# Key transposes one tile in two, earlier key loads and delayed output stores in a hard-max attention kernel

## The chip, the cores and the metric

The kernel runs on one core of one Trainium2 chip. Its time is device microseconds (us) for one execution. Before the change it was 474.49 us (median of 3 runs, 474.13 to 474.59).

Engines: PE is TensorE (PEld its weight loads), DVE is VectorE, ACT is ScalarE, POOL is GpSimd, SP is SyncE.

## The reference

```python
# B=4, Sq=Sk=4096, D=128, float32
logits = np.matmul(q, k.transpose(0, 2, 1))
best = np.argmax(logits, axis=-1)
return v[b_idx, best, :]
```

For each of the 16384 queries, the kernel finds the key with the largest dot product and returns that key's row of v.

## The kernel before

The queries are worked on in 128 tiles of 128 rows, 32 tiles per batch (tile t belongs to batch t // 32). For a tile TensorE makes 4 products of 1024 columns each. `pd` products are differences of key pairs, of which ScalarE takes the absolute value (A); `psn` products are sums to which TensorE then adds A. ScalarE turns the first psn of a tile into E, and VectorE's `fold` combines the second psn with E into W. `top` then takes the eight largest values of W per row.

```python
def dpart(t, x):
    ps = pp.tile([P, 1024], FP32, tag="u", name=f"pd_{t}_{x}")
    mm(ps, t, 1 + 2 * x, True)
    A = ep.tile([P, 1024], FP16, tag=f"A{x}", name=f"A_{t}_{x}")
    nc.scalar.activation(out=A, in_=ps, func=AF.Abs)              # L198
    ...
def spart(t, x):
    ps = pp.tile([P, 1024], FP32, tag="u", name=f"psn_{t}_{x}")
    mm(ps, t, 2 * x, False)                                      # L189
    for n in range(2):
        nc.tensor.matmul(out=ps[...], lhsT=identh, rhs=A[...], start=False, stop=True)   # L208
    if x == 0:
        nc.scalar.activation(out=E, in_=ps, func=AF.Relu, scale=QSCALE)                  # L211
    else:
        E_t[t] = (E_t[t], ps)

def screen(t):          # TensorE's order in one tile
    dpart(t, 0)         # "pd0"
    spart(t - 1, 0)     # "psn0"
    dpart(t, 1)         # "pd1"
    spart(t - 1, 1)     # "psn1"

def fold(t):
    E, ps = E_t.pop(t)
    nc.vector.scalar_tensor_tensor(out=W..., in0=ps, scalar=QSCALE, in1=E,
                                   op0=OP.mult, op1=OP.max)       # L224
```

All these products, and the key transposes, take PSUM buffers from one pool of four, under one tag:

```python
pp = ctx.enter_context(tc.tile_pool(name="ps", bufs=4, space=bass.MemoryType.PSUM))
```

The keys of the next batch must be transposed while this batch runs. This is done in 16 pieces per batch, each of which takes a buffer of the same pool, 8 small matmuls and a copy by ScalarE:

```python
def unit_k(b, i):
    ps = pp.tile([P, 256], FP32, tag="u", name=f"uk_{b}_{i}")
    ...                                                          # matmuls, L163 and L164
    nc.scalar.activation(out=kT[b % 2][:, c:c + 256], in_=ps, func=AF.Copy)   # L167
```

For each tile GpSimd then gathers rows of key differences (`kg`), VectorE makes their dot products (`prod` and what follows), picks the winner, GpSimd gathers the rows of v, and SyncE stores them. Near tiles 80 to 85 a segment of extra work for close cases (the "flags") also takes two PSUM buffers, `fp` and `fq`. The main loop before, cut:

```python
units += [(x - 1, x - NQT + 8 + 3 * i // 2, unit_k, b, i) for i in range(16)]   # from tile 8 of a batch, 2 tiles of 3
for it in range(T):
    b, qt = it // NQT, it % NQT
    if 2 <= qt < 10:
        load_part(b + 1, qt - 2)        # 8 key loads of the next batch
    elif 10 <= qt < 18:
        load_part(b + 1, qt - 2)        # 8 query loads of the next batch
    ...                                 # one transpose unit, if one is due
    if it > 0:
        screen(it)
    if it >= 1:
        fold(it - 1)
    ...
```

## Time and profile before

| | before |
|---|---|
| time, median | 474.49 us |
| profiled span, clock | 472.4 us, 0.944 |
| VectorE busy in 110 us from 30, 140, 250 us | 108.20, 108.11, 108.38 us |
| VectorE's waits, 42 to 420 us | 3.4 us (8 waits) |
| start of the last fold; from there to the end | 419.06 us; 53.3 us |

Two lines from the profile's page of the kernel before: the busy time of each engine over the span (share, instructions), and the group of the fold (busy us, mean ns | idle before it, and what ended most of that).

```profile
PE 381.7 (81%) x1840; PEld 168.9 (36%) x1840; DVE 417.8 (88%) x845; ACT 380.7 (81%) x438; POOL 305.6 (65%) x345
...
L224 DVE SCALAR_TENSOR_TENSOR W<-psn,E 128x1024 int16<-128x1024 f32 x128 | 166.4, 1300 | 15.1 <-ACT E L211 12.1
```

VectorE is the busiest engine, but 88% is an average over a start, a middle and a tail. The windows view of the kernel before shows the middle alone:

```profile
core 0: us, PE busy (x) PEld busy (x) DVE busy (x) ACT busy (x) POOL busy (x), PEclk, DMA share, GB/s
30.00:140.00 110.00, 104.36 (x509) 46.67 (x508) 108.20 (x183) 107.02 (x129) 66.61 (x76) 1.00 0.46 94
140.00:250.00 110.00, 99.89 (x487) 44.63 (x486) 108.11 (x197) 102.23 (x123) 80.14 (x90) 1.00 0.55 117
250.00:360.00 110.00, 99.86 (x475) 43.56 (x473) 108.38 (x217) 101.57 (x117) 78.07 (x81) 1.00 0.43 105
```

VectorE is busy all but 1.6 to 1.9 us of each 110. What it waits for is in the view of waits, here for VectorE from 42 to 420 us in the kernel before (us in total, times, longest):

```profile
DVE W L224 <- PE psn L208: 3.0, 7, 0.9
DVE prod L260 <- DMA kg<-k,cand: 0.4, 1, 0.4
```

So the fold waited 7 times for the psn sum from TensorE, 3.0 us in all, and a dot product once for a gather. VectorE's timeline of the kernel before places them; five of the eight are shown (start, duration; in brackets the idle time before and what ended it):

```profile
164.52 0.56 DVE L260 TENSOR_TENSOR prod<-kg,natq 128x768 f16<-128x768 f16 x1 [0.45 <-DMA kg<-k,cand]
...
176.44 1.30 DVE L224 SCALAR_TENSOR_TENSOR W<-psn,E 128x1024 int16<-128x1024 f32 x1 [0.43 <-PE psn L208]
...
180.03 1.30 DVE L224 SCALAR_TENSOR_TENSOR W<-psn,E 128x1024 int16<-128x1024 f32 x1 [0.39 <-PE psn L208]
...
265.56 1.31 DVE L224 SCALAR_TENSOR_TENSOR W<-psn,E 128x1024 int16<-128x1024 f32 x1 [0.56 <-PE psn L208]
...
283.61 1.30 DVE L224 SCALAR_TENSOR_TENSOR W<-psn,E 128x1024 int16<-128x1024 f32 x1 [0.95 <-PE psn L208]
```

The waits up to 189 us fall where the batch 2 keys are transposed (tiles 40 to 62), those at 241, 266 and 284 us where the batch 3 keys are transposed; at the last two the flags run as well. The Trainium skill (Perfetto Trace Analysis, "Optimization Strategy") says that the same gap repeating on the engine that should be saturated can mean that there isn't enough PSUM for the next tile, and names buffer count and tile sizes.

### The profile page before, as it was taken

Reading aid. Unit: us, or ns where it says so; the run is one execution under the profiler, and the core shown is the slowest. Engines: PE = TensorE matmul, PEld = TensorE weight load, DVE = VectorE, ACT = ScalarE, POOL = GpSimd, SP = SyncE. Lnnn points to the kernel's source line nnn. Section 1 sums busy time; section 2 is a strip of 40 time slices with the busy share of each in tenths; the row PEclk is TensorE's granted clock in tenths of the full one; section 3 lists DMA queues with packets and bytes.
Section 4 is the critical chain, followed back from the end, with each engine's and each line's share of the span. In section 5 each row is a group of like instructions: output and inputs, shape, how many; then the busy total and the mean of one; then the engine's idle time right before and its main releaser. Section 6 shows DMA issues by size and latency. Waiting matters only on the chain. (4 is left out here: it accounts for less than half of the span.)

```text
span 472.4 us, 6274 instructions
## 1 busy us (share of the span) xinstructions
PE 381.7 (81%) x1840; PEld 168.9 (36%) x1840; DVE 417.8 (88%) x845; ACT 380.7 (81%) x438; POOL 305.6 (65%) x345
## 2 busy tenths in 40 slices
PE   7899999999898889999888979999999889920000
PEld 4444444443343334443333434443333333300000
DVE  4288999999999999999999999999999999998400
ACT  1999999999998899999998889999999888920000
POOL 9025544666787876666878765667777567777740
PEclk9999999999999999999999999999999999975555
DMA  7914564143455946242666736142333132324320
GB/s 134 211 32 87 108 115 93 56 119 63 119 94 125 193 87 147 57 124 65 134 133 156 113 108 97 55 114 65 118 89 109 52 94 58 110 73 121 98 82 5
DMA packets 40777, 47.43 MB, mean 100 GB/s; under 512 B 24200, under 2 KB 32395, under 8 KB 40736
## 3 DMA queue, kind: packets, MB, share of 16 engines
q0 software_dynamic: 18464, 30.97, 31.1%
q1 hardware_dynamic: 22272, 16.00, 12.8%
q8 instruction: 15, 0.25, 0.2%
q14 instruction: 26, 0.21, 0.2%
HBM read 39.59 MB, written 12.19 MB: 110 GB/s over the span
## 5 line engine op out<-in xcount | busy, mean ns | idle before, releaser
L198 ACT ACTIVATE A<-pd 128x1024 f16<-128x1024 f32 x256 | 259.1, 1046 | 18.3 <-PE pd L189 17.8
L245 POOL DMA_INDIRECT kg<-k,cand x128 | 127.2, 994 | 103.9 <-DVE p L264 25.0
L224 DVE SCALAR_TENSOR_TENSOR W<-psn,E 128x1024 int16<-128x1024 f32 x128 | 166.4, 1300 | 15.1 <-ACT E L211 12.1
L189 PE MATMUL pd<-kT,qT 128*128 128x512 f16 x512 | 152.1, 378 | 17.4 <-ACT A L198 15.5
L189 PE MATMUL psn<-kT,qT 128*128 128x512 f16 x512 | 151.8, 377 | 15.4 <-ACT A L198 10.8
L189 PEld LDWEIGHTS <-qT 128*128 128x128 f16 x1024 | 98.4, 97 | 166.1 <-issue 77.9
L228 DVE MAX8 TOP<-W 128x8 f32<-128x1024 f32 x128 | 156.2, 1220 | 0.0
L208 PE MATMUL psn<-A,identh 128*128 128x512 f16 x512 | 152.0, 378 | 0.0
L302 POOL DMA_INDIRECT vr<-in_v_dram,win x128 | 125.5, 980 | 39.0 <-issue 35.0
L211 ACT ACTIVATE E<-psn 128x1024 int16<-128x1024 f32 x128 | 132.8, 1038 | 6.7 <-PE psn L208 5.9
L208 PEld LDWEIGHTS <-identh 128*128 128x128 f16 x512 | 49.5, 97 | 60.8
L260 DVE TENSOR_TENSOR prod<-kg,natq 128x768 f16<-128x768 f16 x64 | 35.0, 549 | 1.5 <-DMA kg<-k,cand 1.5
L264 DVE TENSOR_TENSOR p<-prod 128x384 f16<-128x384 f16 x64 | 22.3, 350 | 0.0
L269 DVE TENSOR_REDUCE D<-p 128x6 f32<-128x192 f16 x64 | 21.4, 338 | 0.0
L167 ACT ACTIVATE kT<-uk 128x256 f16<-128x256 f32 x48 | 20.0, 416 | 0.9 <-PE uk L164 0.9
L163 PE MATMUL uk<-identh,natk 128*128 128x128 f16 x96 | 15.8, 218 | 0.6 <-ACT A L198 0.6
L63 POOL DMA_DIRECT2D natk<-in_k_dram x26 | 15.7, 604 | 0.9 <-POOLq L763 0.8
L267 DVE TENSOR_TENSOR p<-p 128x192 f16<-128x192 f16 x64 | 15.7, 247 | 0.0
L66 POOL DMA_DIRECT2D natq<-in_q_dram x26 | 15.4, 594 | 0.1
L460 PE MATMUL fp_e<-n_e,tri 128*128 128x1 f32 x2 | 0.6, 362 | 16.4 <-DVE n_e L458 16.4
L164 PEld LDWEIGHTS <-natk 128*128 128x128 f16 x96 | 9.3, 97 | 7.7 <-issue 5.5
L163 PEld LDWEIGHTS <-natk 128*128 128x128 f16 x96 | 9.3, 97 | 5.6
(148 smaller groups left out, 142.4 us busy)
## 6 DMA issues: line engine op xcount, KB each, us to landing
out_dram<-vr SPq DMA_DIRECT2D x14, 512.0 KB, 3.2
k<-kd SPq DMA_DIRECT2D x8, 384.0 KB, 4.5
natk<-in_k_dram POOLq DMA_DIRECT2D x24, 128.0 KB, 3.8
natq<-in_q_dram POOLq DMA_DIRECT2D x24, 128.0 KB, 3.3
kg<-k,cand POOLq DMA_INDIRECT x128, 2.7
vr<-in_v_dram,win POOLq DMA_INDIRECT x128, 2.5
natk<-in_k_dram POOLq DMA_DIRECT2D x2, 512.0 KB, 7.0
out_dram<-vr SPq DMA_DIRECT2D x4, 256.0 KB, 2.3
```

The costliest lines, as they stand in the source:

```text
L163: nc.tensor.matmul(out=o, lhsT=natk[b % 2][:, h, 4 * m + x, :], rhs=identh, start=True, stop=False)
L189: nc.tensor.matmul(out=ps[:, n * 512:(n + 1) * 512], lhsT=qT[b % 2][:, qt * P:(qt + 1) * P], rhs=kT[b % 2][:, u * 1024 + n * 512:u * 1024 ...
L198: nc.scalar.activation(out=A, in_=ps, func=AF.Abs)
L208: nc.tensor.matmul(out=ps[:, n * 512:(n + 1) * 512], lhsT=identh, rhs=A[:, n * 512:(n + 1) * 512], start=False, stop=True)
L211: nc.scalar.activation(out=E, in_=ps, func=AF.Relu, scale=QSCALE)
L224: nc.vector.scalar_tensor_tensor(out=W_t[t % NW].bitcast(I16)[:, 1::2], in0=ps, scalar=QSCALE, in1=E, op0=OP.mult, op1=OP.max)
L228: nc.vector.max(out=TOP[:, t, :], in_=W_t[t % NW].bitcast(FP32))
L245: near_q.append(lambda j=j: nc.gpsimd.indirect_dma_start(out=kg[:, j].rearrange("p f d -> p (f d)"), out_offset=None, in_=k16[t0 // NQT], ...
L260: nc.vector.tensor_tensor(out=prod, in0=kg, in1=natq[b % 2][:, x - b * NQT:x - b * NQT + m, :].unsqueeze(2).to_broadcast([P, m, 3, P]), op ...
L264: nc.vector.tensor_tensor(out=p1, in0=prod[:, :, :, 0:64], in1=prod[:, :, :, 64:128], op=OP.add)
L269: nc.vector.tensor_reduce(out=d[:, x - c0:x - c0 + m, 1:4], in_=p2, axis=AX_X, op=OP.add)
L302: late_q.append(lambda j=j: nc.gpsimd.indirect_dma_start(out=vr[:, j, :], out_offset=None, in_=v_flat, in_offset=IOA(ap=win[:, j:j + 1], a ...
```

## The change

Its intent is to spread work. The transposes for batches 2 and 3 go over the whole batch before, at one tile in two from its tile 1 on. Those for batch 1 begin at tile 6 instead of 8. The key loads begin sooner (batch 1's at tile 0 instead of 2; those of batches 2 and 3 at tile 18 of the last batch but one, instead of tile 2 of the batch before), and each output store is issued two tiles behind its last gather.

```diff
+    wait_q = []
...
         while late_q and late_q[0] in stores:
-            late_q.pop(0)()
+            wait_q.append((clock[0] + 2, late_q.pop(0)))
+    clock = [0]
+    def put_out(now):
+        while wait_q and wait_q[0][0] <= now:
+            wait_q.pop(0)[1]()
     def issue(it):
         n = 0
+        clock[0] = it
+        put_out(it)
...
-        units += [(x - 1, x - NQT + 8 + 3 * i // 2, unit_k, b, i) for i in range(16)]
+        units += [(x - 1, x - NQT + (6 + 3 * i // 2 if b == 1 else 1 + 2 * i), unit_k, b, i) for i in range(16)]
...
-        if 2 <= qt < 10:
-            load_part(b + 1, qt - 2)
+        if it < 8:
+            load_part(1, it)
         elif 10 <= qt < 18:
             load_part(b + 1, qt - 2)
+        elif 18 <= qt < 26:
+            load_part(b + 2, qt - 18)
...                            # at the end, the last stores are put out at once (late_now)
```

More of the change, by code (lines that the diff above doesn't have):

```diff
@@ L710, in flush, with late_now @@
             near_q.pop(0)()
+    def late_now(n):
+        take_late(n)
+        put_out(1 << 20)
     screen(T)
@@ L746 @@
         drain([p], "cnt" if last else None)
-    flags_last(T // 2, T, lambda: drain([p]), take_late)
+    flags_last(T // 2, T, lambda: drain([p]), late_now)
     man.__exit__(None, None, None)
```

## The prediction

> What bounds the kernel: VectorE. The windows view has it busy 108.2, 108.1 and 108.4 us of the 110 us windows that begin at 30, 140 and 250 us. ScalarE has 101.6 to 107.0, TensorE 99.9 to 104.4, so both have some slack. Outside lie a start (first fold at 19.5 us) and a tail from 420 us, where GpSimd issues gathers back to back (0.94 us and a 0.30 us gap each) until 455 us.
>
> What can be gained. VectorE's waits between 25 and 420 us sum to only about 5.9 us: 2.5 us in the ramp before 40 us (fold waits for ScalarE's E), 0.45 us for a gather at 164.5 us, and seven waits of the fold for TensorE's sum (psn), 2.95 us in all, at 170, 176, 180, 189, 241, 266 and 284 us. Most of these lie where key transposes are made at two tiles of three. A transpose takes one of four PSUM buffers and a ScalarE copy of about 0.4 us; the timeline at 163 to 177 us shows the next matmul waiting about 0.5 us for ScalarE and ScalarE then 0.46 us for that matmul.
>
> What the change moves. Counts stay: 48 transposes, 24 key loads, the same gathers and stores. In batches 2 and 3 the transposes come at one tile in two, so a pause always lies between two; I expect most waits at 170 to 190 us and part of those at 266 and 284 us to go: minus 2 us. The last two also involve the flag segment's PSUM tiles, which stay. Batch 1's transposes begin at tile 6 instead of 8, in the ramp where ScalarE is full (2.75 us per tile, against about 3.05 where VectorE sets the pace): plus 0.5 us.
> Key loads cost GpSimd about 0.58 us and a 0.3 us gap each. Eight leave tiles where GpSimd is full (no slack from 130 to 174 us) for later ones, and eight of batch 3 move to about 72 to 97 us, where GpSimd has about 8 us of slack: the 0.45 us wait may go, nothing else on the critical path.
> The stores' delay frees the sync queue: the store there was followed by bunched query transposes at 179 and 281 us, needed much later: 0. The Trainium skill (DMA: Bandwidth & Descriptors, Issuing engines are not separate DMA queues) says all issuers share the same 16 engines, so it saves no bandwidth; the queues' shares here sum to 44%. One 512 KB store moves into the tail, near the flags' gathers: 0 to plus 0.5 us.
>
> Sum: about minus 2 us, 472.4 us. Range 470.3 to 474.7. Faster by over 2% 0.01, within 2% 0.98, slower 0.01; over 2% would need 9.5 us, more than all of VectorE's waits in that stretch.
>
> What would show it. Waits for psn at 165 to 190 us at most 0.4 us in sum; fold-for-E waits before 45 us larger by about 0.5 us; VectorE's busy total unchanged within 1 us (417.8); last fold about 2 us earlier; time from last fold to end unchanged within 0.7 us; batch-3 key loads at 72 to 97 us.
>
> What would make it wrong. If those waits come from the key differences on VectorE or from late gathers rather than the transposes' density, they stay; if GpSimd, full from 397 us on, sets the end by itself, a VectorE gain is lost; if GpSimd lags in tiles 16 to 26, new gather waits appear.

## More of the kernel before

A buffer holds 1024 float32 (4 KiB) per partition. The Trainium skill (PSUM — Partial Sum Buffer, "PSUM: the matmul accumulator") gives PSUM 16 KiB in each partition, so four such buffers fill it, and a fifth is not to be had; no run here tests that.

## The result, and the profile after

| | before | after |
|---|---|---|
| time, median of 4 runs | 474.54 us (474.13 to 474.59) | 471.19 us (471.06 to 471.39) |
| profiled span, clock | 472.4 us, 0.944 | 469.4 us, 0.941 |
| start of the last fold | 419.06 us | 416.07 us |
| from there to the end | 53.3 us | 53.3 us |

The ratio is 0.9932, with a 95% interval of 0.9914 to 0.9949. The change is worth 3.35 us by the medians.

The same two lines of the page, for the kernel after:

```profile
PE 381.8 (81%) x1840; PEld 169.8 (36%) x1840; DVE 417.2 (89%) x845; ACT 379.7 (81%) x438; POOL 305.8 (65%) x345
...
L224 DVE SCALAR_TENSOR_TENSOR W<-psn,E 128x1024 int16<-128x1024 f32 x128 | 167.6, 1309 | 13.1 <-ACT E L211 11.9
```

No engine has noticeably more or less to do: the totals differ by 1.0 us at most. The idle time before the fold is 2.0 us less. The windows of the kernel after:

```profile
30.00:140.00 110.00, 104.73 (x521) 47.30 (x519) 108.05 (x180) 107.26 (x131) 67.23 (x76) 1.00 0.50 95
140.00:250.00 110.00, 102.09 (x499) 45.62 (x497) 109.21 (x201) 104.20 (x125) 79.42 (x87) 1.00 0.57 114
250.00:360.00 110.00, 100.08 (x465) 43.16 (x464) 110.00 (x221) 101.42 (x115) 79.99 (x83) 1.00 0.47 106
```

VectorE has become full in the third window (110.00) and nearly so in the second (109.21). VectorE's waits from 42 to 420 us in the kernel after:

```profile
DVE W L224 <- PE psn L208: 0.6, 2, 0.3
DVE prod L261 <- DMA kg<-k,cand: 0.2, 1, 0.2
```

Two waits of the fold are left, at 182 and 186 us; those of the flags are gone.

Comparing the starts of the 128 folds in the two traces shows where the time came from. Kernel after minus kernel before: +0.29 us at tile 0, +0.52 at tiles 8 to 47, -0.46 at tiles 56 to 71, -1.57 at tiles 80 to 83, -2.97 from tile 91 on. So the ramp cost 0.23 us, batch 1's tiles gained 0.98 us, and batch 2's tiles (with the flags) 2.5 us. The +0.29 at the first fold is not the change: the run with the stores alone changed, which begins with the same program, had +0.35. The clock between 10 and 15 us differs as well: 1.00 in the profile of before and 0.66 in both others. Over all eight profiles from this chip the two go together: the first fold starts at 19.35 to 19.71 us in the four where that clock is 1.00, and at 19.82 to 19.93 us in the four where it is 0.66 to 0.70. The Trainium skill (TensorE: Matmul & The Clock Gate, Part 1) says that the clock's activity window runs freely, so that the warm-up varies from run to run.

### The profile page after: what moved, and what is told of

Its sections match the earlier page's. It is cut to its first block, busy times and chain, and to the rows that moved or that the text cites. A ratio compares the mean times of both kernels' runs of the same rounds, so it can differ in the third digit from the quotient of the medians.

```text
span 469.4 us, 6266 instructions
## 1 busy us (share of the span) xinstructions
PE 381.8 (81%) x1840; PEld 169.8 (36%) x1840; DVE 417.2 (89%) x845; ACT 379.7 (81%) x438; POOL 305.8 (65%) x345
## 5 line engine op out<-in xcount | busy, mean ns | idle before, releaser
L224 DVE SCALAR_TENSOR_TENSOR W<-psn,E 128x1024 int16<-128x1024 f32 x128 | 167.6, 1309 | 13.1 <-ACT E L211 11.9
L189 PE MATMUL pd<-kT,qT 128*128 128x512 f16 x512 | 152.3, 379 | 15.1 <-ACT A L198 14.4
```

The costliest lines, as they stand in the source:

```text
L189: nc.tensor.matmul(out=ps[:, n * 512:(n + 1) * 512], lhsT=qT[b % 2][:, qt * P:(qt + 1) * P], rhs=kT[b % 2][:, u * 1024 + n * 512:u * 1024 ...
L224: nc.vector.scalar_tensor_tensor(out=W_t[t % NW].bitcast(I16)[:, 1::2], in0=ps, scalar=QSCALE, in1=E, op0=OP.mult, op1=OP.max)
```

## The experiments

The theories are these.

- Density: the waits come because transposes stand at two tiles of three, with too few tiles between them to recover. This is what the prediction said.
- GpSimd: key loads crowd the gathers, so that the rows of key differences arrive late and VectorE's later waits follow from that.
- Stores: output stores held up the sync queue, or moved the tail.
- Buffers (where an expectation says D, it is this one): what matters is which product of a tile is given the PSUM buffer that the fold freed long ago. The framework makes that choice when the program is built, and the change merely made it choose otherwise.

### 1. The parts of the change, one at a time

The key loads alone moved, as in the change, transposes and stores left as before:

```diff
-        if 2 <= qt < 10:
-            load_part(b + 1, qt - 2)
+        if it < 8:
+            load_part(1, it)
         elif 10 <= qt < 18:
             load_part(b + 1, qt - 2)
+        elif 18 <= qt < 26:
+            load_part(b + 2, qt - 18)
```

> The kernel before with only the new key load schedule. Theory A (the waits come from transposes made at two tiles of three): no gain, 474.0 to 475.0 us, VectorE's fold waits for psn between 130 and 290 us still 2 us or more in sum. Theory B (the waits come from GpSimd being full of gathers plus loads): the waits follow the loads; most of the gain appears, 471.5 to 473.0 us, the waits at 165 to 190 us shift to where GpSimd has no slack, those at 241 to 284 us shrink below 0.6 us. Theory C (stores that block the sync queue): no gain, 474.0 to 475.0 us.

Measured: 474.54 us against 474.44 for the kernel before, ratio 1.0005 (0.9992 to 1.0017). VectorE's waits, 42 to 420 us, of this run:

```profile
DVE W L224 <- PE psn L208: 3.3, 7, 1.0
```

The gather wait is gone, and the seven waits of the fold are there as before. The loads alone do nothing for the time.

Loads and transposes as in the change, stores at once as before. The edit is the change with one line's effect taken back:

```diff
-            wait_q.append((clock[0] + 2, late_q.pop(0)))
+            late_q.pop(0)()
```

> The changed kernel without the delayed stores. Theory A and theory B: 471.2 us within 0.4, like the changed kernel. Theory C: 472.5 us or more, with waits for psn just after a store that holds back several query transposes.

Measured: 471.24 us (median of 6 runs, 471.05 to 473.52), ratio 0.9944 (0.9928 to 0.9959). VectorE's waits, 42 to 420 us:

```profile
DVE W L224 <- PE psn L208: 0.8, 3, 0.3
```

This is the change's whole gain: its median lies 0.05 us from the change's own.

The stores alone delayed, loads and transposes as before:

```diff
-            late_q.pop(0)()
+            wait_q.append((clock[0] + 2, late_q.pop(0)))
```

> The kernel before with only the stores issued two tiles behind their last gather. Theories A and B: 474.5 us within 0.4. Theory C: 472.5 us or less, the waits at 180 and 284 us gone. If the tail suffers from the store that moves into it, the time from the last fold to the end grows from 53.3 us by up to 0.5 us.

Measured: 474.81 us, ratio 1.0007 (0.9994 to 1.002). VectorE's waits, 42 to 420 us:

```profile
DVE W L224 <- PE psn L208: 3.4, 7, 1.0
```

The stores are worth nothing.

So, by elimination, the gain belongs to the schedule of the transposes. They were not moved alone: in the change the first transpose for batch 2 comes at tile 33, and the old schedule loads those keys at tiles 34 to 41. The next question is why.

### 2. Is it GpSimd, after all?

The kernel before, with the key and query loads for batches 1 to 3 spread at one tile in two, and the transposes as dense as before:

```diff
-        if 2 <= qt < 10:
-            load_part(b + 1, qt - 2)
-        elif 10 <= qt < 18:
-            load_part(b + 1, qt - 2)
+        if 2 <= it < 10:
+            load_part(1, it - 2)
+        if b >= 1 and qt in (0, 2, 4, 6):
+            load_part(b + 1, 4 + qt // 2)
+        elif 8 <= qt < 24 and qt % 2 == 0:
+            load_part(b + 1, 8 + (qt - 8) // 2)
+        elif qt in (24, 26, 28, 30):
+            load_part(b + 2, (qt - 24) // 2)
```

> The kernel before with its transposes still at two tiles of three and old stores, but with every load of batches 1 to 3 at one tile in two (batch 1's key loads stay as they are), so that GpSimd is never full for long. Theory A: 474.0 to 475.0 us, psn waits between 130 and 290 us still 2 us or more. Theory B: 471.0 to 472.8 us, at most 0.6 us of such waits between 130 and 200 us, and GpSimd keeps some slack in each 10 us of 130 to 200 us.

Measured: 474.65 us, ratio 1.0006 (0.9993 to 1.0019). VectorE's waits, 42 to 420 us:

```profile
DVE W L224 <- PE psn L208: 3.0, 7, 1.0
DVE W L224 <- PE uk L164: 0.4, 1, 0.4
```

The gather no longer waits, but the next fold, at 166.57 us, now waits 0.4 us for TensorE instead, and every fold starts within 0.05 us of where it started before. So the 0.45 us gather wait of the kernel before had hidden a wait for TensorE of the same size: taking it away gains nothing. The GpSimd theory falls.

### 3. What TensorE waits for

The timeline of TensorE in the kernel before, around the transpose of tile 47 (the last line is pd0 of tile 47):

```profile
162.41 0.22 PE L163 MATMUL uk<-identh,natk 128*128 128x128 f16 x1
...
162.57 0.22 PE L164 MATMUL uk<-identn,natk 128*128 128x128 f16 x1
163.30 0.59 PE L189 MATMUL pd<-kT,qT 128*128 128x512 f16 x2 [0.51 <-ACT A L198]
```

And ScalarE at the same time:

```profile
162.23 1.02 ACT L198 ACTIVATE A<-pd 128x1024 f16<-128x1024 f32 x1
163.13 0.39 ACT L167 ACTIVATE kT<-uk 128x256 f16<-128x256 f32 x1
163.99 1.02 ACT L198 ACTIVATE A<-pd 128x1024 f16<-128x1024 f32 x1 [0.46 <-PE pd L189]
```

After the transposes, pd0 of tile 47 waits 0.51 us for ScalarE's A copy, which ends at 162.23 + 1.02 = 163.25 us. pd0 starts 0.05 us later. It waits because it was given the very buffer that this copy was reading. Then ScalarE, whose transpose copy ended at 163.52, stands for 0.46 us until pd0 is there. Two engines wait for each other in turn, and about half a microsecond is lost on both, though a buffer stood free. The built program tells which. These are the buffers (0 to 3) of tile 47's products in the kernel before and in the kernel of section 5, in TensorE's order; the star marks the product that reuses the buffer of the fold of two tiles back (psn_44_1), which had been read long ago:

```
product     before   buffers by hand
uk_2_5      1        2
pd_47_0     2        3 *
psn_46_0    1        0
pd_47_1     3 *      2
psn_46_1    2        3
```

Before, the early buffer goes to pd1, the third product. In the trace TensorE's products follow the order of the program: while pd0 waits 0.51 us, no later product runs, so the early buffer is of no use. If pd0 has it, TensorE runs on at once and ScalarE gets its next input in time (tile 47 of section 5).

Sorting the tiles by which product has the fold's old buffer, the distance between the ends of psn1 of one tile and the next (median us, worked out from TensorE's timeline for tiles 12 to 111; tiles of the flags and a few rarer cases left out) is:

| tile | fold's old buffer goes to | before | after | by hand (section 5) |
|---|---|---|---|---|
| no transpose | psn0 | 2.68 (21 tiles) | 2.71 (28) | 2.75 (53) |
| no transpose | pd1 | 3.05 (21) | 3.07 (15) | - |
| no transpose | psn1 | 3.06 (10) | 3.06 (10) | - |
| with transpose | pd0 | 3.13 (19) | 3.13 (20) | 3.13 (43) |
| with transpose | pd1 | 3.60 (15) | 3.52 (10) | - |
| with transpose | psn0 | 3.59 (6) | 3.60 (9) | - |

VectorE needs about 3.09 us per tile (mean from tile 14 to 78 in the kernel of section 5, where it never waits there). So a good tile without a transpose wins TensorE some 0.4 us of lead, a good one with a transpose is about even (3.13), and a bad one with a transpose loses half a microsecond. In the kernel before, that lead (start of a fold minus the end of its psn1; 0.11 us is a fold that waits) is 1.9 to 2.4 us at tiles 32 to 38, where there are no transposes. From tile 40 on it shrinks, with ups and downs: 0.93 us at tile 43, 0.54 and 0.16 at tiles 46 and 47, and 0.11 at most tiles from 49 to 55. In batch 0, tiles 14 to 31, transposes stand at the same two tiles of three, and yet the lead stays between 1.3 and 2.4 us: there the buffer goes to pd0 in 9 of the 12 tiles with a transpose, and to pd1 in none. That is a first sign against density.

Of the 32 transposes of batches 2 and 3, the buffer goes to pd1 or psn0 in 21 before (15 and 6), in 19 after (10 and 9) and in 16 of the dense version below (9 and 7). (The expectations of the next group quote other counts, 20, 15 and 13, miscounted from the built program.) What differs more is the tiles without a transpose: those of the good kind, with the buffer on psn0, rose from 21 to 28.

This allows an estimate of what the other mix of kinds is worth. Over iterations 33 to 96 of the main loop (32 tiles with and 32 without a transpose in both kernels) TensorE took 205.7 us before and 202.7 after, 3.0 us less, as much as the last fold gained. All but 0.6 us of that is in tiles without a transpose. With the mean time of each kind as before, the change's mix alone would give 3.6 us less (the two slow tiles of the flags left out). It is an account of two traces, not an experiment: the change altered the buffers and the spacing together.

### 4. Buffers by hand, and density, on a disturbed chip

Four kernels tell density and buffers apart. Two have the schedules before or after, with the PSUM buffers of each product fixed by hand so that the fold's old buffer goes to pd0 in tiles with a transpose and to psn0 in others (from tile 11 on). One has the change's schedule with the buffer always given to pd1. One has the change with transposes again two tiles of three, with the framework's choice of buffers. The edit for hand-made buffers, cut (x, y, old: the buffers of psn0 and pd1 of the tile before, and the fold's old one):

```diff
-        ps = pp.tile([P, 1024], FP32, tag="u", name=f"pd_{t}_{x}")
+        ps = ptile(None, f"pd_{t}_{x}", (("A0", "A1")[x], now[0]))   # one of tags u0..u3, bufs=1 each
...
+    def lay(t, has_u):
+        x, y, old, pend = ph
...                                    # uk, (pd0, psn0, pd1, psn1)
+            u, o = (x, (old, y, x, old)) if has_u else (None, (x, old, y, x))      # good
+            u, o = (x, (y, x, old, y)) if has_u else (None, (x, y, old, x))        # bad variant
```

> The kernel before with all its schedules; only the choice of PSUM buffer is made by hand from tile 11 on, so that the buffer which the fold frees goes to a tile's first product (pd, first half) where a transpose is in the tile and to its second (psn, first half) where none is, never to the third. Theory A (density of the transposes): still 474.5 us within 0.5 and psn waits of 2 us or more between 130 and 290 us. Theory D (which product inherits the fold's buffer): 471.2 to 472.6 us, psn waits there at most 1 us in sum, and TensorE takes about 3.1 us per tile with a transpose instead of 3.5 to 3.6.

> The changed kernel with the same choice by hand. Theory A: 471.2 us within 0.4. Theory D: 470.0 to 471.1 us, the waits at 182 and 185 us gone.

> The changed kernel (transposes at one tile in two) with the buffer which the fold frees always given to the third product (pd, second half) from tile 11 on. Theory A: 471.2 us within 0.6. Theory D: 473.5 us or more, psn waits of 2 us or more in sum, in batches 0, 1 and 2 alike, TensorE about 3.5 us per tile with a transpose and 3.1 without.

The dense version: 

```diff
-        units += [(x - 1, x - NQT + (6 + 3 * i // 2 if b == 1 else 1 + 2 * i), unit_k, b, i) for i in range(16)]
+        units += [(x - 1, x - NQT + (6 if b == 1 else 1) + 3 * i // 2, unit_k, b, i) for i in range(16)]
```

> The changed kernel with the transposes of batches 2 and 3 again at two tiles of three, begun at the batch's second tile as in the change; buffers chosen by the framework. In its program 13 tiles of batches 1 and 2 have a transpose and the fold's buffer at the third or (in a tile with a transpose) the second product, against 20 before and 15 in the change. Theory A: 474.0 us or more. Theory D: 471.0 to 473.0 us.

These four ran on another chip, and there the kernel before took 505.49 to 521.46 us, with a clock of 0.92 and stalls of several microseconds at places that are quiet on the first chip. The times:

| run | median us | ratio (95%) |
|---|---|---|
| slots_old: schedule before, buffers good | 516.06 | 1.0127 (1.0013 to 1.0242) |
| slots_new: schedule after, buffers good | 509.1 | 0.9996 (0.9879 to 1.0112) |
| slots_new_bad: schedule after, buffers bad | 521.34 | 1.0238 (1.012 to 1.0355) |
| dense_units: change, transposes dense | 509.78 | 0.9999 (0.9865 to 1.0134) |

With intervals this wide the expected half a per cent cannot be seen, and the verdict on all four is "unclear". Set against before, they do not bear the buffer theory out: the schedule before with good buffers was even slower there. Against each other two of them do: slots_new and slots_new_bad differ in the buffers alone, and their fast runs took 506.48 to 511.40 us with good buffers and 519.18 to 523.80 with bad ones. That is the expected direction, but several times the expected size, so the stalls have a part in it. Otherwise only stretches without a stall can be compared in the traces. From 42 to 100 us neither the kernel before (first chip) nor slots_old has a wait of VectorE; the change with bad buffers has nine:

```profile
DVE W L268 <- PE psn L252: 3.7, 9, 0.8
```

and its timeline shows the pattern already in batch 0, where no other kernel has it:

```profile
56.19 1.31 DVE L268 SCALAR_TENSOR_TENSOR W<-psn,E 128x1024 int16<-128x1024 f32 x1 [0.40 <-PE psn L252]
...
66.43 1.31 DVE L268 SCALAR_TENSOR_TENSOR W<-psn,E 128x1024 int16<-128x1024 f32 x1 [0.67 <-PE psn L252]
```

There the tiles with a transpose took TensorE 3.56 us and those without 3.13 (medians), about as the bad kinds in the table above. In this stretch the transposes stand at two tiles of three, as in the kernel before: so at the same density bad buffers bring the waits into tiles that had none. Later the trace tests the spacing itself. From 120 to 180 us (tiles 33 to 50), without a stall and at a clock of 1.00, transposes stand at one tile in two; with bad buffers tiles with and without one take TensorE 3.52 and 3.13 us in turn, and VectorE is busy for 57.5 us of the 60, against 60.0 with the same spacing in the kernel after (first chip). So the pause between transposes alone does not keep the fold from waiting. In slots_old, with the old density and good buffers, the lead was 1.7 to 3.0 us at tiles 40 to 53. dense_units had stalls of 1.2 and 1.9 us at 111 to 116 us, and then no wait of the fold until the next stall at 211 us, though the lead fell to 0.11 us at tile 51; that is weak evidence that density alone doesn't bring the waits back. The profile of slots_new fell in a slow run and is not used.

A second try, on a third chip, with the schedule before and with the best combination I could think of (the change's loads, stores and transposes, but batch 1's transposes from tile 8 as before, and good buffers):

> Repeat of slots_old, whose chip was disturbed (the kernel before took 505 to 521 us there): old transposes, loads and stores, buffers by hand. Theory A: 474.4 us within 0.5, psn waits 2 us or more between 130 and 290 us. Theory D: 471.2 to 472.6 us, at most 1 us of such waits; what is left sits at the flag segment's tiles near 266 and 284 us.

> The changed kernel with buffers by hand as in slots_new, and batch 1's transposes begun at tile 8 again instead of 6. Theory A: 471.0 us within 0.4. Theory D: 470.0 to 470.9 us, no psn wait between 40 and 260 us. The later start should take 0.2 to 0.5 us out of VectorE's waits between 30 and 42 us in either theory.

That chip was disturbed as well (before: 514.76 to 526.79 us, clock 0.91): 520.91 us, ratio 0.9977 (0.9872 to 1.0083), and 518.95 us, ratio 0.9971 (0.9885 to 1.0057). Both are inconclusive. In slots_old2 the lead of TensorE was 1.4 to 2.7 us at tiles 40 to 53, where before it falls to 0.11.

### 5. The same two kernels on the first chip

The third group of runs got the first chip again, undisturbed (before: 474.8 us, 474.22 to 475.29, 11 runs). The first kernel is the schedule before with every load, store and transpose at its old place, and only the buffers fixed by hand:

> Third try of slots_old, hoping for an undisturbed chip (the kernel before at about 474.5 us; on the two earlier chips it took 505 us and more). Old transposes, loads and stores, buffers by hand. Theory A (density): 474.4 us within 0.5, psn waits 2 us or more between 130 and 290 us. Theory D (which product inherits the fold's buffer): 471.2 to 472.6 us, at most 1 us of such waits. If the chip is disturbed again, only the stretch before its first stall is read: theory A a lead of TensorE under 0.3 us at tiles 47 to 55, theory D 1.5 us or more.

Measured: 471.12 us (median of 6 runs, 469.85 to 472.41), ratio 0.9925 (0.9914 to 0.9937); profiled span 468.1 us, clock 0.941. VectorE has no wait at all from 42 to 420 us. Its windows from 140 us on:

```profile
140.00:250.00 110.00, 103.20 (x504) 46.08 (x503) 110.00 (x202) 105.25 (x126) 81.90 (x92) 1.00 0.56 118
250.00:360.00 110.00, 101.04 (x480) 44.20 (x478) 110.00 (x223) 102.29 (x118) 79.74 (x82) 1.00 0.45 106
```

VectorE is full in both. The median is 0.08 us below the range that the buffer theory gave. What went is TensorE's part of the ring of waits with ScalarE. In the kernel before, the view of waits, 42 to 420 us:

```profile
ACT A L198 <- PE pd L189: 17.8, 39, 0.7
PE pd L189 <- ACT A L198: 15.5, 39, 0.5
```

and with buffers by hand (the same two lines of code, which stand 44 lines further down in that kernel):

```profile
ACT A L242 <- PE pd L233: 6.0, 14, 1.1
...
PE pd L233 <- ACT A L242: 0.6, 2, 0.3
```

TensorE's waits for ScalarE before a pd went from 15.5 us to 0.6. Instead it waits for VectorE: in the same stretch 11.5 us in 29 waits for a fold to free its buffer (8.1 before a psn, 3.4 before a pd), against 0.2 us in the kernel before. TensorE is then as far ahead as the buffers let it be, and ScalarE's remaining 6.0 us cost nothing that this trace shows. The change itself left most of the ring in place. The same view of the kernel after:

```profile
ACT A L198 <- PE pd L189: 17.0, 36, 0.7
PE pd L189 <- ACT A L198: 14.4, 37, 0.5
```

Tile 47 of the kernel with buffers by hand, on TensorE:

```profile
164.22 0.22 PE L208 MATMUL uk<-identn,natk 128*128 128x128 f16 x1
164.27 0.59 PE L233 MATMUL pd<-kT,qT 128*128 128x512 f16 x2
```

pd0 follows the last transpose without a gap. And on ScalarE:

```profile
163.89 1.03 ACT L242 ACTIVATE A<-pd 128x1024 f16<-128x1024 f32 x1
164.79 0.41 ACT L211 ACTIVATE kT<-uk 128x256 f16<-128x256 f32 x1
165.05 1.06 ACT L242 ACTIVATE A<-pd 128x1024 f16<-128x1024 f32 x1
```

ScalarE has no gap either. The lead stays at 1.2 us or more at tiles 40 to 79, with the same dense transposes that took it to 0.11 before. So density is not what makes the fold wait; which product gets which buffer is. A gain as large as the change's (3.7 us by the medians) is had without moving a single transpose. How much of the change's own gain came through the buffers does not follow from this run; for that there are the estimate of section 3 and, on a disturbed chip, slots_new_bad.

The second kernel is slots_best again:

> Second try of slots_best: the changed kernel, buffers by hand, batch 1's transposes begun at tile 8. Theory A: 471.0 us within 0.4. Theory D: 470.0 to 470.9 us, no psn wait between 40 and 260 us. On a disturbed chip only the stretch before its first stall is read.

Measured: 470.04 us (median of 6 runs, 469.43 to 472.69), ratio 0.9909 (0.9889 to 0.9929), span 468.4 us. VectorE again has no wait from 42 to 420 us. By the medians this is the best version, 1.15 us below the change's 471.19; but those two were not run in the same rounds, and their intervals against before (0.9889 to 0.9929, and 0.9914 to 0.9949) overlap. Against slots_old3 of the same rounds it isn't told apart either: the means are 0.6 us apart, the intervals overlap, and its span is 0.3 us longer. Once the buffers are right, then, these runs show no worth of spacing the transposes; they would not rule out some 0.4%. Runs with buffers by hand also scatter more (by 2.6 and 3.3 us) than the change's (0.3 us in 4 runs), though loads_units also had one run at 473.52. In both kernels the slowest run has the lowest clock (472.41 us at 0.937 and 472.69 at 0.933) and the fastest the highest (469.85 at 0.941 and 469.43 at 0.942); the cause is open. slots_old3's profile is of its fastest run, so its trace gains more on before than its median does.

The results of all twelve kernels were correct.

What stays open: why the framework picks the buffers that it picks; how much of the change's own gain comes from another choice of buffers and how much from the rest between transposes, since neither dense_units nor slots_new_bad was ever timed on an undisturbed chip; and whether good buffers by hand help at all in the disturbed state, where the mean clock with them was 0.89 to 0.92 against 0.91 to 0.93 for the kernel before.

## Why the prediction was right or wrong

The predicted time was 472.4 us, the measured one 471.19, within the range; the gain was 3.35 us where about 2 were expected.

What held:

- VectorE bounds the kernel, and its work does not change: its busy total went from 417.8 to 417.2 us. Its waits of 5.9 us lay well below the 9.5 us that make 2%.
- The last fold came earlier by 2.99 us (about 2 predicted), and the time from there to the end stayed (53.3 us in both).
- The stores and the loads were each worth nothing (1.0007 and 1.0005), and no new gather waits appeared at tiles 16 to 26. The feared 0.5 us in the tail did not come.

What was mis-sized or wrong:

- Waits for psn at 165 to 190 us were to be at most 0.4 us; 0.61 us were left, and a gather wait of 0.16.
- "Part of those at 266 and 284 us" was too little. They went entirely, and batch 2's tiles gave 2.5 us of the gain. This term of the sum is the one that made it 1 us too small: with more lead (2.5 to 3.5 us at tiles 73 to 78, against 1.1 to 1.6 before) the fold outlives the two slow tiles of the flags (about 4.5 and 5.3 us of TensorE each).
- The ramp was to cost 0.5 us, as longer waits of the fold for E; it cost 0.23. Those waits did not grow (12.1 us before, 11.9 after, up to 45 us); a fold waited 0.6 us for psn instead. Batch 1's tiles then gained 0.98 us.
- The name of a batch was wrong: the key loads that moved to 71 to 96 us are batch 2's. Batch 3's went to 173 to 195 us.
- The visible waits understate what there is to gain. They sum to 3.4 us, but in the profiles buffers by hand brought the last fold forward by 4.7 us (419.06 to 414.36; by the median times the gain is 3.7). An instruction that waits for nothing starts about 0.1 us before the one ahead of it ends (162.72 + 1.29 = 164.01, and the next begins at 163.91), so each wait costs about 0.1 us more than its bracket says; and 12 folds stood at a lead of 0.11 or 0.12 us, of which only 7 are listed as waiting. The Trainium skill (Perfetto Trace Analysis, "Optimizing Scalar/DVE Operations") has a reason for the overlap: profiled durations include the write acknowledgement, which overlaps with the next instruction. The trace shows the 0.1 us of overlap; no run here shows its reason.

The step that failed is the cause: "In batches 2 and 3 the transposes come at one tile in two, so a pause always lies between two". The prediction had even read the right line, TensorE waiting 0.5 us for ScalarE and ScalarE 0.46 us for TensorE, and taken it as the price of any transpose. It is the price of a transpose whose pd0 inherits the buffer that ScalarE is emptying. With the same density and pd0 on the fold's old buffer, the pair of waits is gone (slots_old3: 15.5 us of TensorE's waits to 0.6, ratio 0.9925); with the pause and bad buffers, VectorE loses 2.5 us of 60 (slots_new_bad, 120 to 180 us), and in batch 0, as dense as before, the fold waits nine times, 3.7 us in all, where before has no wait. Nor did the change end the pair of waits: TensorE still waits 14.4 us for ScalarE before a pd, against 15.5 before. That the time came out within the range is thus in part luck: moving the transposes also changed which product gets which buffer, which the prediction did not consider. By the estimate of section 3 this is enough for the whole gain, but no run on the first chip separates it from the spacing.

## What to carry to other kernels

When an engine waits in a ring with another (each ends the other's idle time, by about the same amount, in some tiles and not in others that do the same work), list which buffer each product reuses and who read it last, before moving work around. TensorE gained from the buffer that was freed early when the first product of a tile with a transpose got it, and not when the third did. With several products of different readers in one pool, it is worth trying to fix by hand which product gets which buffer, as was done here. And when a wait on the bounding engine goes away without any gain, look for the wait behind it.

## What the Trainium skill lacked or had wrong

- Perfetto Trace Analysis, "Optimization Strategy", says that consistent bubbles can mean too few buffers or the wrong size. It lacks a third possibility. Here the count (four) and the size stayed, and fixing which product inherits which buffer removed all of VectorE's waits from 42 to 420 us and took 474.8 us to 471.12.
- Perfetto Trace Analysis, "Matmuls", advises to rotate matmul groups through different PSUM banks. It lacks that the order of rotation matters where readers differ: a tile with a transpose took TensorE 3.13 us with the early buffer on its first product, and 3.60 us with it on the third, at the same number of buffers.
- Perfetto Trace Analysis, "Identifying Dependency Chains", lacks that removing a wait may merely uncover another that ended at the same time: a gather wait of 0.45 us was removed, and a fold waited 0.4 us for TensorE in its place, with every fold at the same time as before within 0.05 us.
- The same page has the overlap of write acknowledgements, but not that visible waits therefore understate the loss: waits of 3.4 us stood for 4.7 us of VectorE's time in the two profiles.
- No page describes the state of the two disturbed chips: the kernel before took 505 to 527 us there, against 474 on the first, with stalls of several microseconds. Its mean clock was 0.91 to 0.93 against 0.94. But in the profiles of the other kernels from those chips the clock is 1.00 from 42 to 100 us, and between there and 420 us it falls below 1.00 where VectorE stalls (slots_old: 0.74 from 340 to 360 us, with VectorE busy for 12.8 us of 20). So the lower mean goes with the stalls. What else ran on those chips is not known; with intervals of about 1% on either side, half a per cent could not be measured there.
